# GLA outputs directly behind the out-projection of the head ahead, next queries, keys and log gates behind them

## The chip, the cores and the metric

The kernel runs on one core of one Trainium2 chip. The metric is device time in microseconds (us) of one execution. Engines are named as in the profile: PE is TensorE (matmuls and transposes; PEld its weight loads), ACT is ScalarE, DVE is VectorE, POOL is GpSimd, SP is SyncE, which issues most DMAs. "L151" is line 151 of the kernel.

## The reference

Two layers of width 1024 on a sequence of 512 tokens: an SSD mixer, then a gated linear attention (GLA) mixer, each behind a root-mean-square norm and added to the residual stream, then a last norm. The change lies in the GLA mixer:

```python
def gla_scan(q, k, v, lg):                       # chunks of 64
    def step(s, inp):
        qc, kc, vc, gc = inp
        cum = jnp.cumsum(gc, axis=1)
        qg = qc * jnp.exp(cum)
        kg = kc * jnp.exp(-cum)
        att = jnp.where(causal, jnp.einsum('blhk,bshk->bhls', qg, kg), 0.0)
        o = jnp.einsum('bhls,bshv->blhv', att, vc) + jnp.einsum('blhk,bhkv->blhv', qg, s)
        kd = kc * jnp.exp(cum[:, -1:] - cum)
        s = s * jnp.exp(cum[:, -1])[..., None] + jnp.einsum('bshk,bshv->bhkv', kd, vc)
        return s, o

def gla_mixer(u, w_in, w_gate, b_gate, onorm, w_out):   # 4 heads, keys 128 wide, values 512
    q, k, v, z, gl = split(u @ w_in)
    lg = log_sigmoid(einsum('bldr,drk->bldk', gl, w_gate) + b_gate) / 16
    o = gla_scan(q, k, v, lg[:, :, 0]) + rev(gla_scan(rev(q), rev(k), rev(v), rev(lg[:, :, 1])))
    o = rmsnorm(o, onorm) * silu(z)
    return o @ w_out
```

## The kernel before

Products are done in three matmuls (`mm3`, L150): each operand is split into a high and a low half, a copy on ScalarE and a difference on VectorE. Weights pass through a stream (`Weights`): a chunk is loaded by SyncE (three raw buffers), split (L89 and L90, or L94 and L95 where it is scaled; three buffers), and used in the fixed order in which it was added. `W.next()` splits up to two chunks ahead.

The GLA layer is a loop over four heads (L1119 to L1127). For each head:

- `vz_part`: values and output gates by seven block products (`pb`, 24 matmuls each, two weight chunks each), which write to the four PSUM buffers `mm` and are freed by copies and additions (L889, L903).
- `att_part`: from the summed log gates `lgc` the decayed queries and keys (L999 to L1024, alternating between ScalarE and VectorE), then the attention of all 512 tokens in both directions at once, with masked blocks (`bd`, `pta`), split into `ah` and `al`.
- `proj_out` of the head ahead (`po`, 96 matmuls), reading `gyh` and `gyl`.
- `qk_part` of the next head (`pch`, 48 matmuls, two chunks).
- `gates` of the next head: two matmuls (`ptg`), then for each direction Abs (L959), min (L960), Exp (L963), Ln (L966), a difference (L968) and a running sum (L970).
- `o_part`: for each of four token tiles twelve matmuls (`pto`), a square with its sum (L1092), the root on GpSimd (L318, L319) and the gated product (L1094); then four transposes (`ptyg`, L1078) and a split into `gyh` (ScalarE, L156) and `gyl` (VectorE, L157).

PSUM has four buffers `mm`, three buffers `wk` (`pta`, `ptg`, `pto`) and one buffer `cb` (`bd`, `ptyg`). `gyh`, `gyl` and `lgc` have one buffer each, `gy` two.

The order of each engine's instructions is not the order of the program. A planner lists them by priority, which is the place in the program, shifted where the code says so: weight splits 60 ahead, squares, products and splits of `o_part` 150 ahead, its transposes 24 behind. An instruction is placed when the planner takes its operands to be ready. On the chip each engine then runs its list in that order.

The lines that the change moves:

Of the kernel before, what the change touches and what calls it, by code (L numbers as in the profile page):

```python
# [13 lines left out]
AF = mybir.ActivationFunctionType  # L14
# [14 lines left out]
GH = 4  # L29
# [100 lines left out]
def build(tc, I, out):  # L130
    nc = tc.nc
    ctx = ExitStack()
    with ctx:
# [7 lines left out]
        def mmb(name):  # L141
            return ps.tile([P, 512], F32, tag="mm", name=name, bufs=4)

        def wkb(name):
            return ps.tile([P, 512], F32, tag="wk", name=name, bufs=3)

        def cbb(name):
            return ps.tile([P, 512], F32, tag="cb", name=name, bufs=1)

        def mm3(pt, a, b, first, last):  # L150
            nc.tensor.matmul(pt, lhsT=a[0], rhs=b[0], start=first, stop=False)  # L151
            nc.tensor.matmul(pt, lhsT=a[0], rhs=b[1], start=False, stop=False)  # L152
            W.mm = nc.tensor.matmul(pt, lhsT=a[1], rhs=b[0], start=False, stop=last)  # L153

        def split(hi, lo, src):
            nc.scalar.copy(hi, src)  # L156
            nc.vector.tensor_tensor(out=lo, in0=src, in1=hi.bitcast(F32), op=ALU.subtract)  # L157
# [94 lines left out]
        class Blocks:  # L252
# [8 lines left out]
            def step(self, n):  # L261
                w = self.w
                dst, src, add = (
                    (w["w1"], self.b11, False),
                    (w["w3"], self.b12, False),
                    (w["w1"], self.b12, True),
                    (w["w3"], self.b22, True),
                    (w["w2"], w["w1"], False),
                    (w["w2"], self.b22, True),
                    (w["w4"], w["w2"], False),  # L270
                    (w["w4"], self.b21, True),
                )[n]
                if add:
                    dma = nc.gpsimd.dma_start(dst, src, accum_op=ALU.add)
                else:
                    dma = nc.gpsimd.dma_start(dst, src)
                tc.add_manual_dep(
                    dma.ins, W.mark.ins.name,
                    mybir.DependencyInfo(mybir.DependencyClass.Sync, mybir.DependencyReason.DATA),
                    reason="pace",  # L280
                )
# [35 lines left out]
        def rms(dst, ss, mul, add):  # L317
            nc.gpsimd.tensor_scalar(out=dst, in0=ss, scalar1=mul, scalar2=add, op0=ALU.mult, op1=ALU.add)  # L318
            nc.gpsimd.tensor_tensor(out=dst, in0=dst, in1=nhalf[:, 0 : dst.shape[-1]], op=ALU.pow)  # L319
# [37 lines left out]
        def proj_ch(m=P):  # L357
            wh, wl = W.next()
            pt = mmb("pch")
            for k in range(KD):  # L360
                mm3(pt[0:m], (wh[k], wl[k]), (uh[:, k], ul[:, k]), k == 0, k == KD - 1)
            return pt
# [14 lines left out]
        def proj_out(yts, step=lambda: None):  # L377
            for hf in range(2):
                pts = [mmb(f"po{t}") for t in range(NT)]
                for kk in range(2):  # L380
                    if hf or kk:
                        step()
                    wh, wl = W.next()
                    for t in range(NT):
                        for j in range(2):
                            k = 2 * kk + j
                            mm3(pts[t], yts(k, t), (wh[j], wl[j]), k == 0, k == 3)
                for t in range(NT):
                    hs = h[t][:, hf * 512 : (hf + 1) * 512]
                    nc.vector.tensor_tensor(out=hs, in0=hs, in1=pts[t], op=ALU.add)  # L390
# [49 lines left out]
        with tc.tile_pool(name="sp", bufs=1, reuse_waits="tile") as sp:  # L440
# [347 lines left out]
            zs = {}  # L788
# [37 lines left out]
        with tc.tile_pool(name="gp", bufs=1, reuse_waits="tile") as gp:  # L826
# [124 lines left out]
            def gates(hd):  # L951
                lgc = gp.tile([P, 2, L], F32, tag="lgc", name=f"lgc{hd}")
                ab = []
                for d in range(2):
                    b = bgT[:, d * 4 + hd : d * 4 + hd + 1]
                    pt = wkb("ptg")
                    nc.tensor.matmul(pt, lhsT=wgs[d][:, hd * P : (hd + 1) * P], rhs=gl, start=True, stop=True)
                    a = gp.tile([P, L], F32, tag="ee", name=f"ab{d}", bufs=2)
                    nc.scalar.activation(a, pt, AF.Abs, bias=b)  # L959
                    nc.vector.tensor_scalar(  # L960
                        out=lgc[:, d], in0=pt, scalar1=b, scalar2=0.0, op0=ALU.add, op1=ALU.min
                    )
                    nc.scalar.activation(a, a, AF.Exp, scale=-1.0)  # L963
                    ab.append(a)
                for a in ab:
                    nc.scalar.activation(a, a, AF.Ln, bias=1.0)  # L966
                for d, a in enumerate(ab):
                    nc.vector.tensor_tensor(out=a, in0=lgc[:, d], in1=a, op=ALU.subtract)  # L968
                    lv, av = (lgc[:, d], a) if d == 0 else (lgc[:, d, ::-1], a[:, ::-1])
                    nc.vector.tensor_tensor_scan(  # L970
                        out=lv, data0=rmf, data1=av, initial=0.0, op0=ALU.mult, op1=ALU.add
                    )
                return lgc

            def b4(t):
                return t.rearrange("p (c l) -> p c l", l=P)

            def qk_part(hd):
                q = gp.tile([P, L], F32, tag="q", name=f"q{hd}", bufs=1)
                k = gp.tile([P, L], F32, tag="k", name=f"k{hd}", bufs=1)  # L980
                nc.scalar.mul(q, proj_ch(), float(P) ** -0.5)
                nc.scalar.copy(k, proj_ch())
                return q, k
# [82 lines left out]
            def o_part(hd, att, vs, zs):  # L1066
                yh = gp.tile([P, 4, L], F32R, tag="gyh", name=f"gyh{hd}")
                yl = gp.tile([P, 4, L], F32R, tag="gyl", name=f"gyl{hd}")
                yg[hd] = (yh, yl)
                ys = {}  # L1070

                def trans(t):
                    y = ys.pop(t)
                    sl = slice(t * P, (t + 1) * P)
                    pt = cbb("ptyg")
                    with tc.high_priority(offset=-YG_BEHIND):
                        for f in range(4):
                            nc.tensor.transpose(pt[:, f * P : (f + 1) * P], y[:, f * P : (f + 1) * P], idn)  # L1078
                    with tc.high_priority(offset=YG_AHEAD):
                        split(yh[:, :, sl], yl[:, :, sl], b4(pt))  # L1080

                for t in range(NT):
                    sl = slice(t * P, (t + 1) * P)
                    po = wkb("pto")
                    for J in range(4):
                        ah, al = att[J]
                        mm3(po, (ah[:, sl], al[:, sl]), vs[J], J == 0, J == 3)
                    y = gp.tile([P, 512], F32, tag="gy", name="gy", bufs=2)
                    ss = gp.tile([P, 1], F32, tag="ss", name="ss", bufs=3)
                    rs = gp.tile([P, 1], F32, tag="rs", name="rs", bufs=3)  # L1090
                    with tc.high_priority(offset=YG_AHEAD):
                        nc.scalar.activation(y, po, AF.Square, accum_out=ss)  # L1092
                        rms(rs, ss, 1.0 / 128, 4 * EPS)
                        nc.vector.scalar_tensor_tensor(  # L1094
                            out=y, in0=po, scalar=rs, in1=zs[t // 2][:, t % 2], op0=ALU.mult, op1=ALU.mult
                        )
                    ys[t] = y
                    if t:
                        trans(t - 1)
                trans(NT - 1)  # L1100

            def yts2(hd):
                def f(k, t):
                    yh, yl = yg[hd]
                    sl = slice(t * P, (t + 1) * P)
                    return yh[:, k, sl], yl[:, k, sl]

                return f
# [10 lines left out]
            for hd in range(GH):  # L1119
                vs, zs = vz_part(*([first] if hd == 0 else []))  # L1120
                att = att_part(lgc, *qk)
                if hd:
                    proj_out(yts2(hd - 1))
                if hd + 1 < GH:
                    qk = qk_part(hd + 1)
                    lgc = gates(hd + 1)
                o_part(hd, att, vs, zs)  # L1127
            nb3 = gp.tile([P, D], F32, tag="lgc", name="nb3")
            nc.gpsimd.dma_start(nb3, I["final_norm"].partition_broadcast(P))
            part = {}  # L1130
# [57 lines left out]
```

## Time and profile before

| | us |
|---|---|
| median of three runs | 888.52 |
| lowest and highest | 884.68 and 890.88 |
| profiled execution | 888.3 |
| its span, first to last instruction | 886.6 |
| TensorE busy | 845.9 |
| VectorE busy | 679.4 |
| ScalarE busy | 507.9 |

The mean granted clock of TensorE over the span is 0.989 of full speed. The GLA layer takes the time from about 500 us to the end. Busy time of TensorE is modelled at its end: a matmul of 512 columns is shown with 0.39 us, while the next starts 0.23 us later. So rates are read from starts.

### The profile page before, as it was taken

Reading aid. Unit: us, or ns where it says so; the run is one execution under the profiler, and the core shown is the slowest. Engines: PE = TensorE matmul, PEld = TensorE weight load, DVE = VectorE, ACT = ScalarE, POOL = GpSimd, SP = SyncE. Lnnn points to the kernel's source line nnn. Section 1 sums busy time; section 2 is a strip of 40 time slices with the busy share of each in tenths; the row PEclk is TensorE's granted clock in tenths of the full one; section 3 lists DMA queues with packets and bytes.
Section 4 is the critical chain, followed back from the end, with each engine's and each line's share of the span. In section 5 each row is a group of like instructions: output and inputs, shape, how many; then the busy total and the mean of one; then the engine's idle time right before and its main releaser. Section 6 shows DMA issues by size and latency. Waiting matters only on the chain.

```text
span 886.6 us, 11281 instructions
## 1 busy us (share of the span) xinstructions
PE 845.9 (95%) x3982; PEld 691.4 (78%) x3982; DVE 679.4 (77%) x1046; ACT 507.9 (57%) x1076; POOL 92.8 (10%) x156
## 2 busy tenths in 40 slices
PE   8998989999999999997999999989999999999996
PEld 5787868788887788886887767868887788878875
DVE  6498978999668987568897789878955885588644
ACT  4337687956666466546565547586526653575233
POOL 2002011101001011001101320010001000110012
PEclk9999999999999999998999999999999999999999
DMA  6547856858877687686431236405522453246202
GB/s 207 138 118 280 206 163 194 247 136 262 188 212 214 167 240 191 182 241 166 131 97 58 66 104 186 124 24 162 171 75 69 141 167 95 72 143 189 73 1 95
DMA packets 90198, 132.92 MB, mean 150 GB/s; under 512 B 7969, under 2 KB 49149, under 8 KB 87966
## 3 DMA queue, kind: packets, MB, share of 16 engines
q1 hardware_dynamic: 78716, 97.46, 35.4%
q0 software_dynamic: 11424, 34.74, 16.8%
q8 instruction: 31, 0.51, 0.2%
q14 instruction: 25, 0.20, 0.1%
q10 hardware_dynamic: 2, 0.00, 0.0%
HBM read 129.96 MB, written 35.78 MB: 187 GB/s over the span
## 4 chain that ended last, share of the span: by engine, by line
PE 67%; DVE 11%; ACT 11%; DMA 4%; issue 4%; POOL 3%; SPq 0%; POOLq 0%; ACTq 0%; DVEq 0%
PE po L151 5%; PE po L152 5%; PE pch L152 5%; PE po L153 5%; PE pch L151 5%; PE pch L153 5%; PE pb L151 4%; PE pb L152 4%; PE pb L153 4%; PE pyi L709 3%; DMA bct<-cumd 3%; PE ptk L151 3%; PE ptk L152 3%; PE ptk L153 3%; DVE wlo L90 2%
## 5 line engine op out<-in xcount | busy, mean ns | idle before, releaser
L89 ACT CAST whi<-wraw 128x1024 fp32r<-128x1024 f32 (+1 forms) x114 | 118.7, 1041 | 137.2 <-PE pb L153 43.5
L90 DVE TENSOR_TENSOR wlo<-wraw,whi 128x1024 fp32r<-128x1024 f32 (+1 forms) x114 | 140.4, 1234 | 73.5 <-ACT whi L89 72.9
L151 PE MATMUL pch<-uh,whi 128*128 128x512 f32 (+2 forms) x336 | 133.3, 397 | 0.0
L153 PE MATMUL pch<-uh,wlo 128*128 128x512 f32 (+2 forms) x336 | 132.7, 395 | 0.6 <-DVE wlo L90 0.5
L152 PE MATMUL pch<-ul,whi 128*128 128x512 f32 (+2 forms) x336 | 132.7, 395 | 0.0
L153 PEld LDWEIGHTS pch<-uh,wlo 128*128 128x128 f32 (+2 forms) x336 | 62.6, 186 | 14.9 <-DVE wlo L90 1.5
L152 PEld LDWEIGHTS pch<-ul,whi 128*128 128x128 f32 (+2 forms) x336 | 62.8, 187 | 13.8 <-issue 0.3
L151 PEld LDWEIGHTS pch<-uh,whi 128*128 128x128 f32 (+2 forms) x336 | 62.8, 187 | 13.4
L541 DVE SCALAR_TENSOR_TENSOR cv<-pch,colA,cv 128x511 f32<-128x511 f32 (+1 forms) x96 | 70.7, 742 | 0.3
L94 ACT ACTIVATE whi<-wraw,colB 128x512 fp32r<-128x512 f32 x58 | 39.0, 716 | 53.7 <-PE pch L152 30.0
L318 POOL TENSOR_SCALAR rs<-ss 128x2 f32<-128x2 f32 (+1 forms) x32 | 11.8, 369 | 434.4 <-ACT gy L1092 323.1
L668 ACT ACTIVATE bct<-bct,eb 128x128 f32<-128x128 f32 x128 | 41.3, 392 | 22.0 <-DMA bct<-cumd 22.0
L151 PE MATMUL ptk<-whi,uh 128*128 128x512 f32 x128 | 51.8, 405 | 0.0
L95 DVE SCALAR_TENSOR_TENSOR wlo<-wraw,colB,whi 128x512 fp32r<-128x512 f32 x58 | 41.8, 747 | 11.8 <-ACT whi L94 11.2
L152 PE MATMUL ptk<-wlo,uh 128*128 128x512 f32 x128 | 50.8, 398 | 0.0
L153 PE MATMUL ptk<-whi,ul 128*128 128x512 f32 x128 | 50.6, 396 | 0.0
L676 ACT ACTIVATE bct<-bct,eb 128x128 f32<-128x128 f32 x128 | 41.2, 391 | 6.5 <-DVE bct L673 6.5
L151 PE MATMUL pb<-whi,uh 128*128 128x512 f32 x96 | 39.7, 414 | 2.0 <-DVE u L889 2.0
L707 ACT ACTIVATE xc<-xt,coef 128x64 f32<-128x64 f32 x128 | 33.7, 337 | 10.8 <-DVE coef L629 10.7
L153 PE MATMUL pb<-whi,ul 128*128 128x512 f32 x96 | 39.9, 415 | 0.0
L152 PE MATMUL pb<-wlo,uh 128*128 128x512 f32 x96 | 39.4, 410 | 0.0
L390 DVE TENSOR_TENSOR h<-h,po 128x512 f32<-128x512 f32 x48 | 32.0, 683 | 9.0 <-PE po L153 9.0
(309 smaller groups left out, 2042.0 us busy)
## 6 DMA issues: line engine op xcount, KB each, us to landing
wraw<-in_ssd_w_in_dram SPq DMA_DIRECT2D x48, 512.0 KB, 5.5
wsumw<-in_gla_w_in_dram POOLq DMA_DIRECT2D x24, 1024.0 KB, 9.6
bct<-cumd SPq DMA_DIRECT2D x16, 1024.0 KB, 6.5
wraw<-in_gla_w_in_dram SPq DMA_DIRECT2D x32, 512.0 KB, 3.7
wraw<-wsumw SPq DMA_DIRECT2D x32, 512.0 KB, 3.6
wraw<-in_ssd_w_out_dram SPq DMA_DIRECT2D x16, 512.0 KB, 4.1
wraw<-in_gla_w_out_dram SPq DMA_DIRECT2D x16, 512.0 KB, 3.9
h<-in_x_dram SPq DMA_DIRECT2D x4, 512.0 KB, 7.8
```

What stands on the lines that cost most here:

```text
L89: self.mark = nc.scalar.copy(vh, raw)
L90: nc.vector.tensor_tensor(out=vl, in0=raw, in1=vh.bitcast(F32), op=ALU.subtract)
L94: self.mark = nc.scalar.mul(hs[j], raw[:, j], g)
L95: nc.vector.scalar_tensor_tensor(out=ls[j], in0=raw[:, j], scalar=g, in1=hs[j].bitcast(F32), op0=ALU.mult, op1=ALU.subtract)
L151: nc.tensor.matmul(pt, lhsT=a[0], rhs=b[0], start=first, stop=False)
L152: nc.tensor.matmul(pt, lhsT=a[0], rhs=b[1], start=False, stop=False)
L153: W.mm = nc.tensor.matmul(pt, lhsT=a[1], rhs=b[0], start=False, stop=last)
L390: nc.vector.tensor_tensor(out=hs, in0=hs, in1=pts[t], op=ALU.add)
L541: nc.vector.scalar_tensor_tensor(out=cv[:, o0:o1], in0=pt[:, o0 + s : o1 + s], scalar=cwt(j, a), in1=cv[:, o0:o1], op0=ALU.mult, op1=ALU.add,)
L668: nc.scalar.activation(bct[:, r], bct[:, r], AF.Identity, bias=TM["eb"][:, cc, i : i + 1])
L676: nc.scalar.activation(et[:, r], et[:, r], AF.Exp, bias=TM["eb"][:, cc, i : i + 1])
L707: nc.scalar.mul(xc[:, q, k], xt[:, cc, k], coef[:, cc, r : r + 1])
```

## The change

Two edits. In the loop over heads, `o_part` of heads 1 and 2 moves from behind the next queries, keys and gates to directly behind `proj_out`; in head 0, which has no out-projection ahead, it moves to between `qk_part` and `gates`. Head 3 stays as it is. In `gates`, an order is laid on ScalarE: the two Ln follow the second Exp (`issue_after` makes an instruction follow another in the list of its engine).

```diff
@@ gates
-                    nc.scalar.activation(a, a, AF.Exp, scale=-1.0)
+                    last = nc.scalar.activation(a, a, AF.Exp, scale=-1.0)
                     ab.append(a)
                 for a in ab:
-                    nc.scalar.activation(a, a, AF.Ln, bias=1.0)
+                    with tc.issue_after(last.ins):
+                        last = nc.scalar.activation(a, a, AF.Ln, bias=1.0)
@@ loop over heads
                 att = att_part(lgc, *qk)
                 if hd:
                     proj_out(yts2(hd - 1))
+                    o_part(hd, att, vs, zs)
                 if hd + 1 < GH:
                     qk = qk_part(hd + 1)
+                if not hd:
+                    o_part(hd, att, vs, zs)
+                if hd + 1 < GH:
                     lgc = gates(hd + 1)
-                o_part(hd, att, vs, zs)
```

## Rows read from the trace of the kernel before

**Rows 1.** The page, its first section: busy time, share of the span and instructions of each engine.

```profile
PE 845.9 (95%) x3982; PEld 691.4 (78%) x3982; DVE 679.4 (77%) x1046; ACT 507.9 (57%) x1076; POOL 92.8 (10%) x156
```

**Rows 2.** The timeline of TensorE from 545 to 866 us, rows that have idle time ahead of them (in brackets, with what released them; one such row, of the last out-projection, is left out). Columns: start, duration, engine, line, operation, output and input, shapes, count.

```profile
549.11 0.47 PE L151 MATMUL pb<-whi,uh 128*128 128x512 f32 x1 [2.01 <-DVE u L889]
...
597.48 0.66 PE L1078 MATMUL ptyg<-idn,gy 128*128 128x128 f32 x4 [3.20 <-DVE gyl L157]
...
687.86 0.33 PE L1078 MATMUL ptyg<-idn,gy 128*128 128x128 f32 x1 [1.45 <-DVE gyl L157]
...
691.66 0.66 PE L1078 MATMUL ptyg<-idn,gy 128*128 128x128 f32 x4 [0.17 <-DVE gyl L157]
...
778.97 0.33 PE L1078 MATMUL ptyg<-idn,gy 128*128 128x128 f32 x1 [1.45 <-DVE gyl L157]
...
863.35 0.66 PE L1078 MATMUL ptyg<-idn,gy 128*128 128x128 f32 x4 [0.20 <-DVE gyl L157]
```

**Rows 3.** The timeline of TensorE behind two of these stalls: the first and the last of eight matmuls in a row from 550.40 on, and of nine from 597.89 on.

```profile
550.40 0.63 PE L153 MATMUL pb<-whi,ul 128*128 128x512 f32 x1
...
553.39 0.53 PE L151 MATMUL pb<-whi,uh 128*128 128x512 f32 x1
...
597.89 0.64 PE L152 MATMUL pb<-wlo,uh 128*128 128x512 f32 x1
...
601.32 0.46 PE L151 MATMUL pb<-whi,uh 128*128 128x512 f32 x1
```

**Rows 4.** The timeline of TensorE: the first and the last of the 48 matmuls of queries and keys of head 2.

```profile
660.76 0.39 PE L151 MATMUL pch<-uh,whi 128*128 128x512 f32 x1
...
671.42 0.39 PE L153 MATMUL pch<-uh,wlo 128*128 128x512 f32 x1
```

**Rows 5.** The timeline of ScalarE, with one row of TensorE, from the gates of head 1 to the split of the first output tile of head 0.

```profile
580.85 1.28 ACT L966 ACT_TABLE_LOAD   x1
...
582.79 1.28 ACT L963 ACT_TABLE_LOAD   x1
...
585.31 1.28 ACT L966 ACT_TABLE_LOAD   x1
...
587.25 1.28 ACT L999 ACT_TABLE_LOAD   x1
...
591.60 0.60 PE L1078 MATMUL ptyg<-idn,gy 128*128 128x128 f32 x4
...
595.47 0.63 ACT L1003 ACTIVATE ee<-cm 128x512 f32<-128x512 f32 x1 [1.35 <-DVE cm L1000]
596.01 0.57 ACT L156 CAST gyh<-ptyg 128x512 fp32r<-128x512 f32 x1
```

**Rows 6.** The same place in head 1: the last transpose of the first output tile and what ScalarE did then.

```profile
684.29 0.27 PE L1078 MATMUL ptyg<-idn,gy 128*128 128x128 f32 x1
...
686.08 0.53 ACT L1023 ACTIVATE cm<-cm 128x384 f32<-128x384 f32 x1 [0.28 <-DVE cm L1020]
686.51 0.57 ACT L156 CAST gyh<-ptyg 128x512 fp32r<-128x512 f32 x1
```

**Rows 7.** The same place in head 3, the last head.

```profile
854.17 0.60 PE L1078 MATMUL ptyg<-idn,gy 128*128 128x128 f32 x4
...
854.80 0.59 ACT L156 CAST gyh<-ptyg 128x512 fp32r<-128x512 f32 x1 [1.12 <-PE ptyg L1078]
```

**Rows 8.** The timelines of VectorE and GpSimd: the last low half of the attention of head 1, and the first root of head 3's outputs.

```profile
644.19 0.69 DVE L157 TENSOR_TENSOR al<-pta,ah 128x512 fp32r<-128x512 f32 x1 [0.65 <-ACT ah L156]
...
846.81 0.18 POOL L318 TENSOR_SCALAR rs<-ss 128x1 f32<-128x1 f32 x1 [58.03 <-ACT gy L1092]
```

**Rows 9.** Instructions by line: those of the gates over the whole trace (duration in ns as least/median/most, first and last start in us), and, from the groups of VectorE between 683.26 and 726.07 us (busy us, mean ns, idle before), those of the outputs.

```profile
L959 ACT ACTIVATE ab<-ptg,colB x8: 689/696/714, 532.9 to 764.7; 128x512 f32<-128x512 f32 x8
L963 ACT ACTIVATE ab<-ab x8: 632/638/647, 534.1 to 765.8; 128x512 f32<-128x512 f32 x8
L963 ACT ACT_TABLE_LOAD  x1: 1283/1283/1283, 582.8 to 582.8; - x1
L966 ACT ACTIVATE ab<-ab x8: 622/632/633, 537.5 to 769.6; 128x512 f32<-128x512 f32 x8
L960 DVE TENSOR_SCALAR lgc<-ptg,colB x8: 742/744/751, 534.5 to 765.6; 128x512 f32<-128x512 f32 x8
L968 DVE TENSOR_TENSOR ab<-lgc,ab x8: 668/686/693, 538.6 to 772.3; 128x512 f32<-128x512 f32 x8
L970 DVE TENSOR_TENSOR_SCAN lgc<-rmf,ab x8: 1217/1220/1226, 540.3 to 773.5; 128x512 f32<-128x512 f32 x8
...
L157 DVE TENSOR_TENSOR gyl<-ptyg,gyh 128x512 fp32r<-128x512 f32 x4 | 2.7, 685 | 0.0
L1094 DVE SCALAR_TENSOR_TENSOR gy<-pto,rs,zs 128x512 f32<-128x512 f32 x2 | 1.5, 752 | 0.8 <-POOL rs L319 0.7
```

**Rows 10.** Busy time of each engine in two stretches that lie behind the `pto` matmuls of head 1. Columns: stretch, length, busy us (instructions) of PE, PEld, DVE, ACT and POOL, granted clock, DMA share, GB/s.

```profile
683.26:698.00 14.74, 13.12 (x65) 10.07 (x64) 13.24 (x22) 12.34 (x25) 2.19 (x4) 1.00 0.24 72
698.00:714.53 16.53, 16.53 (x74) 13.69 (x73) 11.69 (x15) 7.37 (x8) 0.00 (x0) 1.00 0.63 188
```

**Rows 11.** The same view of a stretch in head 0, and the VectorE addition in its timeline that released TensorE at 549.11.

```profile
540.00:550.00 10.00, 7.99 (x36) 6.34 (x35) 10.00 (x14) 7.33 (x12) 0.00 (x0) 1.00 0.68 191
...
548.27 1.28 DVE L889 TENSOR_TENSOR u<-pb,u 128x512 f32<-128x512 f32 x2
```

## Prediction

> **What bounds the kernel now.** I read the page first: TensorE is busy for 845.9 us, 95% of the span, VectorE 77% [rows 1]. So time can be won only where TensorE stands still or runs slowly. Next came TensorE's order of time through the GLA layer, keeping only instructions with idle time in brackets [rows 2]. After 545 us there are few, and all but the first are four transposes (`ptyg`, L1078) waiting for `gyl`, the low half of the transposed output of the token tile ahead. All `ptyg` share one PSUM buffer (`cbb`, one buffer), so the transposes of tile t wait until ScalarE (`gyh`) and VectorE (`gyl`) have emptied it of tile t-1. The stalls: 3.20 us in head 0 (597.48), 1.45 and 0.17 us in head 1 (687.86, 691.66), 1.45 us in head 2 (778.97). Head 3 has 0.20 us (863.35).
>
> The first stall costs more than its idle time. Nine matmuls start from 597.89 to 601.32, (601.32-597.89)/8 = 0.43 us apart [rows 3]. In the projection of queries and keys 48 start between 660.76 and 671.42, (671.42-660.76)/47 = 0.227 us apart [rows 4]. The former is the lower of the clock's two levels (1.2 against 2.4 GHz). It costs 8 x (0.43-0.227) = 1.6 us, 1.7 with the four transposes before them. After the 1.45 us stalls the matmuls show no such slowing. What can be won is 3.20 + 1.7 + 1.45 + 0.17 + 1.45 = **8.0 us**.
>
> Then I asked why `gyl` is late: what do ScalarE and VectorE do meanwhile? In head 0, transposes of tile 0 start at 591.60 and take 0.60 us, but `gyh` starts only at 596.01. Ahead of it ScalarE has exponentials of the next head's attention (L1003 at 595.47, itself idle 1.35 us for VectorE), and before these four table loads of 1.28 us at 580.85, 582.79, 585.31 and 587.25, because L963 (Exp) and L966 (Ln) alternate [rows 5]. In head 1 it is the same on a smaller scale: the last transpose of tile 0 starts at 684.29, `gyh` at 686.51, behind L1023 of the next attention at 686.08, which waited for VectorE [rows 6]. In head 3, where nothing of a next head is left, transposes at 854.17 are followed by `gyh` at 854.80 [rows 7]. So the log gates, and the next attention that they release, stand in the way of the outputs.
>
> **The change part by part.**
>
> *Order of heads 1 and 2.* Before: out-projection of the head ahead, queries and keys of the next (48 matmuls, 11.1 us), gates (2 matmuls), outputs. After: out-projection, outputs (48 `pto` matmuls and 16 transposes), queries and keys, gates. No instruction is added or dropped. Can the outputs start 11 us earlier? They need the attention halves `ah`, `al`; the last `al` of head 1 is made at 644.19 and the out-projection runs to 660.76 [rows 4, 8], so 16 us are to spare. They also overwrite `gyh`/`gyl`, which the out-projection reads (one buffer each), but the first such write is a whole `pto` stage later. The tail of the outputs (in head 3 from the first transposes at 854.17 to the last at 863.35, 9.2 us [rows 2, 7]) now lies beside 11 us of query and key matmuls that need two weight splits, and gates and next attention can't get ahead of it, since they follow these matmuls. What is left is head 3's figure, 0.20 us each. Gain: 1.45 + 0.17 + 1.45 - 2 x 0.20 = **2.7 us**.
>
> *Head 0.* Here the outputs pass only the gates. Its `pto` wait for the last `al`, and before, matmuls of the next block product and the gates' two filled that time; now block matmuls alone do, and two chunks of them are split ahead. I cost this at nothing; at worst the gates' two matmuls are not replaced (0.5 us). The squares of tiles 0 and 1 find ScalarE free. Those of 2 and 3 still fall among the gates. The delay left is one activation or one table load, 0.6 to 1.3 us (L963 0.638, load 1.283 [rows 5, 9]); between nothing and head 1's 1.45 I take 0.8. A stall this short left the clock up in head 1, so the slow stretch goes too. Gain: 3.20 + 1.7 - 0.8 = **4.1 us**.
>
> *Both Exp, then both Ln.* Where they alternated (head 0 only) two of the four loads go: 2 x 1.28 = 2.6 us of ScalarE, none of it TensorE time in itself, so zero in the sum; it is inside the 0.8 above. Only one L963 in the whole trace has a load of its own [rows 9], so the other heads have them paired already. The price is that the first Ln waits for the second Exp, thus for the second gate matmul; behind it queue the `gyh` of tiles 1 to 3. They have higher priority (offset 150) and are planned ahead, so I add nothing; at worst this is one load, 1.3 us.
>
> The rows say that Exp and Ln need a load between them, every time. The Trainium skill, ScalarE: Activation LUTs, section "Table sets: the hidden batching unit", says one set holds both, so that Ln after Exp would need no second load. By that the pairing would remove nothing, and head 0 would keep some 2.6 us more delay: gain 4.2 instead of 6.8. The trace disagrees (four loads in 6.4 us), and I follow the trace.
>
> *What arrives at the front of the next block products.* Gates and next attention now compete with weight splits there. From 683.26 to 714.53 VectorE was busy 13.24 + 11.69 = 24.9 of 31.3 us [rows 10]. Out go four `gyl` (2.7) and two L1094 (1.5). In come the gates' two each of L960, L968, L970: 2 x (0.744 + 0.686 + 1.220) = 5.3, less a scan mostly there already (about 1), and a difference of the next attention (L1000, as long as an L968: 0.7) [rows 9]. Net +0.8: 5.6 us stay idle. On ScalarE, 12.34 + 7.37 = 19.7 us, plus 2 x (0.696 + 0.638 + 0.632) + 2.6 = 6.5, less four `gyh` of 0.57 [rows 5]: 23.9. It fits on average, and weight splits keep their priority. Bounds for a head: nothing, as in this stretch of heads 1 and 2 today, or what head 0 pays for gates inside block products. There, VectorE fully busy from 540 to 550, the addition L889 that should free PSUM came at 548.27, TensorE idled 2.01 us, and then eight matmuls started from 550.40 to 553.39, 0.43 us apart, 7 x 0.2 = 1.4 us lost: 3.4 us in all [rows 2, 3, 11]. Head 0 has the splits of the sums of `u` on top, so I take nothing.
>
> DMA: the order of weights is unchanged (outputs use none); the loads of SyncE's queue stay paced by buffers, three deep. On GpSimd L318/L319 move earlier; its one later item is the load of `final_norm` (L1129), which waits for the last gates' buffer and comes later by about the 11 us that they do. Before head 3's L318 at 846.81 that engine has 58.03 us of idle time [rows 8], so it has room.
>
> **Sum.** 2.7 + 4.1 = 6.8 us. The profiled execution took 888.3 us (span 886.6 and 1.7 around it), 0.2 under the median of the three runs, so it stands for them. 888.3 - 6.8 = **881.5 us**, 0.8% less.
>
> **Rivals.**
>
> *A. Head 0 keeps its stall.* If the planner (which fills each engine's order by priority, that is the order of the program shifted by the offsets) still puts the gate matmuls ahead of the last `pto`, as filler while `al` is awaited, gates stay in front of the squares. Against: three `wk` buffers are taken by `pta` and `pto` first. Only heads 1 and 2 gain: 888.3 - 2.7 = 885.6.
>
> *B. Slower: gates and attention clog the front of the block products.* Price: head 0's 3.4 us, in heads 1 to 3: 10.2 - 6.8 = +3.4, 891.7. It decides once an L889 or L90 is queued behind a VectorE step that waits for ScalarE for longer than two block chunks (24 matmuls x 0.227 = 5.4 us). For it: L1003 and L1023 already hold up `gyh` in this way. Against: 5.6 us of slack, and no stall in those stretches now. The Trainium skill, TensorE: Matmul & The Clock Gate, section "Architectural detail: the array is 16× 32×32, not 1× 128×128", says both engines take strictly what is first in the queue. `gyh` behind L1003 agrees with that.
>
> *C. Not what it says.* The transposes are planned by priority (24 behind); if they are simply drawn forward too, the wait for `gyl` recurs among the query matmuls: 888.
>
> *D. More.* The 3.4 us at 549 also vanish because the new edges shift the gates of head 0: 878.1. Nothing in the diff aims at it.
>
> **How the numbers follow.** Forecast 0.58, A 0.14, B 0.13, C 0.08, D 0.07. The three runs lie 0.7% apart, so 1% is about what a measurement can tell from no change. Below 879.6: D, and the forecast with all residues gone (880.3) on a good run: 0.14. Above 897.2: only B with longer stalls: 0.06. Range 878 to 890: it leaves out B and half of D.
>
> **What would show it.** In the new trace: no idle time above 0.5 us on `ptyg` in heads 1 and 2; `gyh` within 1 us of its transposes; ptyg among `pch`; two loads instead of four in head 0's gates; no matmuls 0.43 us apart near 600. It would be wrong if block matmuls (`pb`) that wait for L889 or L90 appear in the 30 us after the gates, or if `pto` of head 1 starts later than its out-projection ends.

## The result and the profile after

The changed kernel takes 880.16 us (median of six runs, 878.35 to 882.64), the kernel before 887.19 (six runs, 884.68 to 890.88): ratio 0.992, 95% interval 0.9899 to 0.9941, so 0.8% less, 7.0 us. Forecast were 881.5 us and 6.8 us. A second measurement of the changed kernel (`e9_after`, below) gave 0.9922 [0.9897, 0.9947].

The page of the profile after, its first lines:

```profile
span 880.3 us, 11269 instructions
PE 845.4 (96%) x3982; PEld 691.6 (79%) x3982; DVE 677.9 (77%) x1046; ACT 505.2 (57%) x1074; POOL 89.3 (10%) x156
```

The span shows 6.3 us of the difference; what lies ahead of the first gate matmul, mostly the SSD layer, took about 1.1 us more in this profiled execution, and the change doesn't touch it. So the two traces are compared over the GLA stretch, from the first gate matmul (`ptg` of head 0) to the end of the last matmul: 349.7 us before and 342.2 us after, 7.5 us less. The columns of these rows, before and after, are those of [rows 10]:

```profile
529.86:879.59 349.73, 340.43 (x1544) 277.64 (x1544) 252.88 (x360) 187.86 (x304) 20.70 (x43) 0.99 0.36 110
...
531.01:873.24 342.23, 338.43 (x1544) 276.41 (x1544) 251.13 (x360) 184.74 (x302) 17.26 (x43) 1.00 0.37 113
```

TensorE's idle time in it went from 9.3 to 3.8 us, and its busy time is 2.0 us less: the slow matmuls went, at the same number of instructions. (Over the whole span busy time differs by only 0.5 us, since the part ahead of the stretch took longer.)

The timeline of TensorE after, again rows with idle time ahead from 545 us on (one row, in the last out-projection, is left out as in [rows 2]):

```profile
550.25 0.47 PE L151 MATMUL pb<-whi,uh 128*128 128x512 f32 x1 [2.01 <-DVE u L889]
...
799.70 0.47 PE L151 MATMUL pb<-whi,uh 128*128 128x512 f32 x1 [0.83 <-ACT whi L89]
...
857.00 0.66 PE L1079 MATMUL ptyg<-idn,gy 128*128 128x128 f32 x4 [0.21 <-DVE gyl L157]
```

Of the six rows of [rows 2] the four waits of transposes in heads 0 to 2 are gone altogether, with the slow matmuls behind the first [rows 3]; the wait in head 0's own block products and head 3's 0.21 us are as they were. One is new: 0.83 us in head 3, ahead of its sixth block product. The account: 3.20 + 1.7 + 1.45 + 0.17 + 1.45 - 0.83 = 7.1 of the 7.5 us; the rest has no row of its own.

Why the waits went, in head 1: the last transpose of tile 0 and the split behind it, then the same in head 0 with the gates' Exp and Ln (TensorE and ScalarE timelines).

```profile
669.53 0.27 PE L1079 MATMUL ptyg<-idn,gy 128*128 128x128 f32 x1
669.84 0.59 ACT L156 CAST gyh<-ptyg 128x512 fp32r<-128x512 f32 x1 [6.01 <-PE ptyg L1079]
...
590.45 0.49 PE L1079 MATMUL ptyg<-idn,gy 128*128 128x128 f32 x3
591.24 0.58 ACT L156 CAST gyh<-ptyg 128x512 fp32r<-128x512 f32 x1
592.29 0.64 ACT L963 ACTIVATE ab<-ab 128x512 f32<-128x512 f32 x1
593.54 0.63 ACT L963 ACTIVATE ab<-ab 128x512 f32<-128x512 f32 x1
596.19 1.28 ACT L967 ACT_TABLE_LOAD   x1
602.48 1.28 ACT L1000 ACT_TABLE_LOAD   x1
```

In head 1 ScalarE had been idle for 6.01 us when the transposes came, where in [rows 6] the split started 2 us after them. In head 0 `gyh` follows within 0.3 us (4 us late in [rows 5]), and two table loads are left of four.

The new wait, in the timelines of ScalarE and VectorE ahead of 799.70:

```profile
796.64 1.05 ACT L89 CAST whi<-wraw 128x1024 fp32r<-128x1024 f32 x1 [1.85 <-DMA wraw<-wsumw]
797.60 0.63 ACT L1004 ACTIVATE ee<-cm 128x512 f32<-128x512 f32 x1
797.73 1.22 DVE L90 TENSOR_TENSOR wlo<-wraw,whi 128x1024 fp32r<-128x1024 f32 x1 [0.90 <-ACT whi L89]
798.13 0.51 ACT L1010 ACTIVATE e<-lgc 128x384 f32<-128x384 f32 x1
798.54 1.03 ACT L89 CAST whi<-wraw 128x1024 fp32r<-128x1024 f32 x1
798.87 1.28 DVE L889 TENSOR_TENSOR u<-pb,u 128x512 f32<-128x512 f32 x2
```

The row of TensorE names L89 as releaser, which can only be the split at 798.54. But counted through the stream, that split is of the seventh product's first chunk; the two of the sixth were split at 793.34 and 796.64. What fits is the addition L889 at 798.87, which frees PSUM: TensorE starts 0.83 us after it, as it starts 0.84 us after the L889 at 548.27 [rows 11]. That addition stood behind L90 at 797.73, which waited 0.90 us for the split at 796.64, and this for its load. SyncE had issued the load at 791.34, when VectorE had finished the low half (L90, 790.10, 1.21 us) that frees its raw buffer. That the busier VectorE frees the raw buffers later, and so delays the load, is a reading that no experiment tested. The wait is no accident of one execution: the other two traces with this order of heads have it too (0.86 us in `e4_order`, 1.14 us in `e9_after`), and no other trace has it.

### The profile page after: what moved, and what is told of

It reads as the page before. It is cut to its first block, busy times and chain, and to the rows that moved or that the text cites. A ratio compares the mean times of both kernels' runs of the same rounds, so it can differ in the third digit from the quotient of the medians.

```text
span 880.3 us, 11269 instructions
## 1 busy us (share of the span) xinstructions
PE 845.4 (96%) x3982; PEld 691.6 (79%) x3982; DVE 677.9 (77%) x1046; ACT 505.2 (57%) x1074; POOL 89.3 (10%) x156
## 4 chain that ended last, share of the span: by engine, by line
PE 69%; DVE 9%; ACT 8%; DMA 6%; issue 4%; POOL 3%; POOLq 0%; ACTq 0%; DVEq 0%; SPq 0%
DMA bct<-cumd 5%; PE pch L152 5%; PE pch L151 5%; PE pch L153 5%; PE po L151 4%; PE po L152 4%; PE po L153 4%; PE pb L151 4%; PE pb L153 4%; PE pb L152 4%; PE pyi L709 3%; PE ptk L151 3%; PE ptk L153 2%; PE ptk L152 2%; DVE wlo L90 2%
## 5 line engine op out<-in xcount | busy, mean ns | idle before, releaser
L90 DVE TENSOR_TENSOR wlo<-wraw,whi 128x1024 fp32r<-128x1024 f32 (+1 forms) x114 | 140.3, 1233 | 52.3 <-ACT whi L89 52.0
L89 ACT CAST whi<-wraw 128x1024 fp32r<-128x1024 f32 (+1 forms) x114 | 118.5, 1040 | 95.2 <-PE pch L152 28.9
L668 ACT ACTIVATE bct<-bct,eb 128x128 f32<-128x128 f32 x128 | 41.3, 391 | 23.9 <-DMA bct<-cumd 23.7
L318 POOL TENSOR_SCALAR rs<-ss 128x2 f32<-128x2 f32 (+1 forms) x32 | 8.2, 258 | 379.5 <-ACT gy L1093 270.2
L153 PE MATMUL pb<-whi,ul 128*128 128x512 f32 x96 | 38.1, 397 | 0.0
L153 PE MATMUL po<-whi,yl 128*128 128x512 f32 x96 | 38.0, 396 | 0.0
```

The source lines that it names most:

```text
L89: self.mark = nc.scalar.copy(vh, raw)
L90: nc.vector.tensor_tensor(out=vl, in0=raw, in1=vh.bitcast(F32), op=ALU.subtract)
L668: nc.scalar.activation(bct[:, r], bct[:, r], AF.Identity, bias=TM["eb"][:, cc, i : i + 1])
```

## Experiments

All are compared with the kernel before, measured beside them (median 888.55 us for the first four, 887.20 for the next four, 886.69 for the last three). "Stretch" is the GLA stretch of one profiled execution, as above. It also holds or lacks the slow matmuls behind the wait at 549 us, which come and go from one execution to the next (last section): the traces of `e3_ln` and `e6_gates_early` lack them, so about 1.6 us of what their stretch is shorter is chance.

**One part at a time.** The first has only heads 1 and 2 in the new order:

```diff
                 if hd:
                     proj_out(yts2(hd - 1))
+                    o_part(hd, att, vs, zs)
                 if hd + 1 < GH:
                     qk = qk_part(hd + 1)
                     lgc = gates(hd + 1)
-                o_part(hd, att, vs, zs)
+                if not hd:
+                    o_part(hd, att, vs, zs)
```

> Only heads 1 and 2 get the new order (outputs directly behind the out-projection); head 0 and the Exp/Ln order stay as before. Theory (the gates and the next attention stood between the transposes and their split): the waits of the transposes in heads 1 and 2 go, 1.45 + 0.17 + 1.45 = 3.1 us, less up to 0.8 us that the whole change has anew in head 3 at its seventh block product: 2.3 to 3.1 us faster, ratio 0.9965 to 0.9974; head 0's 3.2 us stays. Rival (the paired Exp and Ln is what counts): no change, 1.000.

The second has only head 0 in the new order:

```diff
                 if hd + 1 < GH:
                     qk = qk_part(hd + 1)
+                if not hd:
+                    o_part(hd, att, vs, zs)
+                if hd + 1 < GH:
                     lgc = gates(hd + 1)
-                o_part(hd, att, vs, zs)
+                if hd:
+                    o_part(hd, att, vs, zs)
```

> Only head 0 gets the new order (outputs ahead of the gates); heads 1 and 2 and the Exp/Ln order stay as before. Theory: the 3.20 us wait and the 1.7 us of slow matmuls behind it go, 4.9 us, ratio 0.9945, and the 1.45 us waits of heads 1 and 2 stay, though Exp and Ln may alternate with four table loads as before. Rival (the two table loads are what makes head 0 late): 2 us or more of the wait stay, ratio 0.997 or above.

The third has only the Exp/Ln edit:

```diff
-                    nc.scalar.activation(a, a, AF.Exp, scale=-1.0)
+                    last = nc.scalar.activation(a, a, AF.Exp, scale=-1.0)
                     ab.append(a)
                 for a in ab:
-                    nc.scalar.activation(a, a, AF.Ln, bias=1.0)
+                    with tc.issue_after(last.ins):
+                        last = nc.scalar.activation(a, a, AF.Ln, bias=1.0)
```

> Only both Exp, then both Ln; the order of the heads stays as before. Theory: ScalarE saves two loads of 1.28 us in head 0, but the next attention's exponentials still stand ahead of the split, so 1.5 us or more of the 3.20 us wait stay: 0 to 2.6 us faster, ratio 0.997 to 1.000. Rival: the wait and the slow matmuls go entirely, 4.9 us, ratio 0.9945. Heads 1 and 2 keep 1.45 us each by both.

The fourth has the new order of all heads without that edit (shown against the changed kernel):

```diff
-                    with tc.issue_after(last.ins):
-                        last = nc.scalar.activation(a, a, AF.Ln, bias=1.0)
+                    nc.scalar.activation(a, a, AF.Ln, bias=1.0)
```

> The new order of all heads without the Exp/Ln edit. Theory: within 0.5 us of the whole change, ratio 0.992, with no wait of a transpose over 0.5 us; head 0 may show up to four table loads among the splits. Rival: only heads 1 and 2 gain, ratio 0.9965, and a wait of 2 us or more is left in head 0.

| | median, us | ratio, 95% interval | stretch, us | waits in head 0 (transposes; L889 of head 1's products) | in heads 1 and 2 |
|---|---|---|---|---|---|
| before | 888.55 | | 349.7 | 3.20, slow matmuls | 1.45 + 0.17, 1.45 |
| `e1_heads12` | 883.56 | 0.9949 [0.9932, 0.9965] | 345.9 | 3.19, slow matmuls | none |
| `e2_head0` | 884.05 | 0.9950 [0.9931, 0.9968] | 346.9 | 0.87; 1.02 | 1.45, 1.44 |
| `e3_ln` | 883.74 | 0.9953 [0.9934, 0.9971] | 344.1 | 0.77 | 1.44, 1.44 |
| `e4_order` | 880.95 | 0.9926 [0.9908, 0.9945] | 344.3 | 0.84; 1.02 | none |

Some rows of TensorE's timeline on which the table rests: of `e3_ln` (first), of `e2_head0` (next two), of `e4_order` (last two).

```profile
592.73 0.66 PE L1079 MATMUL ptyg<-idn,gy 128*128 128x128 f32 x4 [0.77 <-DVE gyl L157]
```

```profile
599.73 0.44 PE L1078 MATMUL ptyg<-idn,gy 128*128 128x128 f32 x2 [0.87 <-DVE gyl L157]
620.94 0.47 PE L151 MATMUL pb<-whi,uh 128*128 128x512 f32 x1 [1.02 <-DVE u L889]
```

```profile
601.52 0.66 PE L1078 MATMUL ptyg<-idn,gy 128*128 128x128 f32 x4 [0.84 <-DVE gyl L157]
622.72 0.47 PE L151 MATMUL pb<-whi,uh 128*128 128x512 f32 x1 [1.02 <-DVE u L889]
```

Heads 1 and 2 do what the theory said: their waits of 1.45 us go with their own order and not with the other parts. The 0.17 us of head 1 is in no trace but the first, in those of the old order either (`e2_head0`, `e3_ln`), so it can't be put down to the order. By time `e1_heads12` gained 5.0 us, more than the 2.3 to 3.1 expected (the ratio expected, 0.9965, is the end of the interval); by the trace it is 3.8 us against 3.1, and 0.7 us have no row of their own.

Head 0 is where the theory missed. The Exp/Ln edit alone takes 3.20 us down to 0.77 and the slow matmuls away: 2.4 + 1.7 = 4.1 us. The theory had 1.5 us or more staying. Its ratio, 0.9953, lies outside the 0.997 to 1.000 expected, though the interval reaches into it. ScalarE's timeline of `e3_ln`:

```profile
575.61 0.40 PE L957 MATMUL ptg<-gl,wgs 96*128 96x512 f32 x1
...
579.72 1.28 ACT L967 ACT_TABLE_LOAD   x1
...
582.82 1.28 ACT L1000 ACT_TABLE_LOAD   x1
...
589.76 0.60 PE L1079 MATMUL ptyg<-idn,gy 128*128 128x128 f32 x4
590.23 0.52 ACT L1024 ACTIVATE cm<-cm 128x384 f32<-128x384 f32 x1 [0.37 <-DVE cm L1021]
590.66 0.57 ACT L156 CAST gyh<-ptyg 128x512 fp32r<-128x512 f32 x1
...
592.64 0.64 ACT L1004 ACTIVATE ee<-cm 128x512 f32<-128x512 f32 x1
```

The first gate matmul and the transposes of tile 0 are TensorE's. The first gate matmul before:

```profile
577.40 0.39 PE L957 MATMUL ptg<-gl,wgs 96*128 96x512 f32 x1
```

Steps of the next attention still stand ahead of `gyh`, as the theory had it. But `gyh` comes 3.6 us earlier against the first gate matmul (590.66 - 575.61 = 15.1 us; before 596.01 - 577.40 = 18.6), and so 0.3 us after its transposes. Two things account for it. The two loads are 2 x 1.28 = 2.6 us. And the list is another: the last exponential ahead of `gyh` in [rows 5] (L1003, idle for 1.35 us and 0.54 us from its start to that of `gyh`, 1.9 in all) now stands behind it, as L1004 at 592.64. About 0.9 us is lost again between the other steps, mostly to VectorE. No run has one of the two without the other, so what the loads alone are worth stays open; the 4.1 us belong to the edit.

The new order alone (`e2_head0`, `e4_order`) also takes most: it leaves 0.84 to 0.87 us at a transpose and brings 1.02 us for L889. In `e2_head0` the addition L889 which ends that wait starts 31.4 us after the first gate matmul of head 1 (620.11 - 588.76), in the trace after 29.3 (619.48 - 590.14). That the two loads more, 2.6 us, are what makes it late is argued from this. The waits of head 0 with the slow matmuls are thus 4.9 us with neither edit, 0.8 with the pairing, 1.9 with the order, none with both. The two edits treat one wait; their gains don't add. By time `e4_order` is as expected, and 0.9926 can't be told from the 0.9920 and 0.9922 of the whole change: the 1.9 us that the pairing takes off on top of the order are seen in the traces alone, where waits of no more than 0.5 us were expected.

**What of the order matters.** The changed kernel, with head 0's order in heads 1 and 2 as well:

```diff
                 if hd:
                     proj_out(yts2(hd - 1))
-                    o_part(hd, att, vs, zs)
                 if hd + 1 < GH:
                     qk = qk_part(hd + 1)
-                if not hd:
-                    o_part(hd, att, vs, zs)
+                o_part(hd, att, vs, zs)
                 if hd + 1 < GH:
                     lgc = gates(hd + 1)
```

> The changed kernel, but heads 1 and 2 get head 0's order too: out-projection, next queries and keys, outputs, next gates. The tail of the outputs then lies beside block products, as before the change, and only the gates are out of its way. Theory (gates and next attention in the way are the whole cause): no wait of a transpose above 0.5 us in heads 1 and 2, ratio 0.991 to 0.993, as the changed kernel. Rival (the query and key matmuls beside the tail are what counts): 1.45 us come back in each of heads 1 and 2, ratio 0.9955.

The changed kernel, with the gates in front of the outputs in heads 1 and 2:

```diff
                 if hd:
                     proj_out(yts2(hd - 1))
+                    if hd + 1 < GH:
+                        lgc = gates(hd + 1)
                     o_part(hd, att, vs, zs)
                 if hd + 1 < GH:
                     qk = qk_part(hd + 1)
                 if not hd:
                     o_part(hd, att, vs, zs)
-                if hd + 1 < GH:
                     lgc = gates(hd + 1)
```

> The changed kernel, but in heads 1 and 2 the next gates go between the out-projection and the outputs; queries and keys stay behind the outputs, so the gates stand in front of the outputs again, while the next attention can't start. If the steps of the attention are what holds up the split: waits of the transposes in heads 1 and 2 stay under 0.5 us, ratio 0.991 to 0.993. If the gates are: 0.6 to 1.5 us in each of heads 1 and 2, ratio 0.994 to 0.9955.

Measured: `e5_qk_first` 878.75 us, 0.9913 [0.9895, 0.9931], stretch 341.3; `e6_gates_early` 878.86 us, 0.9913 [0.9892, 0.9933], stretch 339.6. Neither has a wait of a transpose in heads 0 to 2, nor the 0.83 us of head 3. By time neither can be told from the changed kernel. So the query and key matmuls as cover are not needed. And in `e6_gates_early` gates ahead of the outputs do no harm. Head 1 of it, ScalarE's timeline with the last transpose of tile 0:

```profile
658.18 1.28 ACT L967 ACT_TABLE_LOAD   x1
...
661.81 1.28 ACT L1000 ACT_TABLE_LOAD   x1
...
666.82 0.19 ACT L1000 ACTIVATE eT<-lgc 128x4 f32<-128x4 f32 x1
667.45 0.27 PE L1079 MATMUL ptyg<-idn,gy 128*128 128x128 f32 x1
667.75 0.59 ACT L156 CAST gyh<-ptyg 128x512 fp32r<-128x512 f32 x1 [0.74 <-PE ptyg L1079]
```

The gates are over before the transposes come; the attention has run only the steps that need no queries or keys, and the split is on time. So in heads 1 and 2 it was the next attention, with its products of queries and keys, that stood ahead of the split.

**The single PSUM buffer.** The kernel before, one edit:

```diff
-                pt = cbb("ptyg")
+                pt = wkb("ptyg")
```

> The kernel before with one edit: the transposes write to the three PSUM buffers of the attention products instead of the single one. Theory: the single buffer only passes on the lateness of the split; with three buffers the waits for the split go in heads 1 and 2 (1.45 us each) and shrink in head 0, but the outputs' matmuls now share the buffers and may wait: ratio 0.992 to 0.999. Rival (the lateness of ScalarE and VectorE alone sets the time): waits of the same sum appear at the outputs or at the next use of the buffers, ratio 1.000.

Measured 885.27 us, 0.9984 [0.9969, 0.9999], stretch 348.0. The waits move: rows of its TensorE timeline from heads 0 and 1.

```profile
593.73 0.50 PE L151 MATMUL pto<-vh,ah 128*128 128x512 f32 x1 [1.23 <-DVE gyl L157]
...
683.60 0.50 PE L151 MATMUL pto<-vh,ah 128*128 128x512 f32 x1 [1.04 <-DVE gyl L157]
691.24 0.63 PE L1078 MATMUL ptyg<-idn,gy 128*128 128x128 f32 x4 [0.57 <-DVE gy L1094]
```

Head 0 has four waits of 0.91 + 0.44 + 1.23 + 0.87 = 3.45 us in place of 3.20, and no slow matmuls behind any of them; heads 1 and 2 have 1.6 us each. The stretch is 1.7 us shorter, as much as the slow matmuls. The late split sets the waits, the buffer only where they are paid, as the rival said; the expected range holds the ratio all the same.

**A faster version.** The wait at 549 us (L889) is for PSUM. The products of q5 and s3 hold all four buffers until the additions behind s3 are done. With s3 ahead, its buffers are emptied while q5 runs:

```diff
-                p5 = block_mm("q5")
                 p7 = block_mm("s3")
                 u3 = [add(keep(i, "u3"), p7[i], u2[i]) for i in two]
+                p5 = block_mm("q5")
...
-                for src in (self.b11, self.b21, w["w2"], w["w1"], w["w3"], w["w4"], self.b22)[a:b]:
+                for src in (self.b11, self.b21, w["w2"], w["w3"], w["w1"], w["w4"], self.b22)[a:b]:
```

On the changed kernel:

> The changed kernel with the fourth and fifth of the seven block products swapped (their weight chunks too): the product of s3 ahead of that of q5, so that its PSUM buffers are emptied while the product of q5 runs. Theory: the wait of 2.01 us for L889 in head 0 is one for PSUM buffers that both products hold; it goes, with the 1.4 us of slow matmuls behind it, and perhaps the 0.83 us of head 3: 2 to 4 us less than the changed kernel, ratio 0.988 to 0.990. Rival (VectorE has too much to do there): a wait of 1.5 us or more appears at a neighbouring product, ratio 0.992.

The same with the early gates of `e6_gates_early`, beside the changed kernel as it is:

> The changed kernel with the two block products swapped and, in heads 1 and 2, the next gates between the out-projection and the outputs. Theory: the gains of the swap (3 to 4 us over the changed kernel) and of earlier gates add up, since the gates no longer press on the front of the block products: ratio 0.986 to 0.989, fastest of all. Rival: the earlier gates give nothing that the swap has not given, ratio 0.989.

> The changed kernel as it is, beside the next two on the same chip. Theory: ratio 0.991 to 0.994 again, and the 0.83 us wait of head 3 (a weight chunk that landed late) may be there or not; no wait of a transpose in heads 0 to 2.

And on the kernel before:

> The kernel before with the two block products swapped and nothing else. Theory: the wait at 549 us and the waits of the transposes are independent: 2.0 to 3.5 us faster, ratio 0.996 to 0.998, and the 3.20 and 1.45 us waits of the transposes stay. Rival: what TensorE gains in head 0 is given back at the transposes of head 0, ratio 1.000.

| | median, us | ratio, 95% interval | stretch, us |
|---|---|---|---|
| `e7_swap` | 875.19 | 0.9886 [0.9865, 0.9907] | 339.1 |
| `e9_after` | 880.49 | 0.9922 [0.9897, 0.9947] | 342.5 |
| `e10_swap_gates` | 876.45 | 0.9883 [0.9860, 0.9906] | 338.4 |
| `e11_swap_only` | 886.44 | 0.9991 [0.9970, 1.0012] | 349.1 |

TensorE's timeline of `e7_swap` has these rows in place of the wait of 2.01 us, its slow matmuls and the 0.83 us:

```profile
560.02 0.91 PE L1042 MATMUL pta<-sc,sc 128*128 128x128 f32 x6 [1.13 <-DVE sc L1007]
...
719.66 0.71 PE L1043 MATMUL pta<-sc,sc 128*128 128x128 f32 x3 [0.29 <-DVE sc L1025]
...
809.39 1.57 PE L1043 MATMUL pta<-sc,sc 128*128 128x128 f32 x8 [0.56 <-DVE sc L1025]
```

Against the trace after, the stretch is 3.1 us less: 0.9 us of idle time (2.01 + 0.83 gone, 1.13 + 0.29 + 0.56 new at the attention, which waits for VectorE) and 2.2 us of busy time (336.2 against 338.4), with the slow matmuls gone. The ratio is in the range expected. The buffers explain the wait; that VectorE is short of time there is true too. Early gates give nothing that can be told from what the swap has given, as the rival said: 0.9883 against 0.9886. Beside `e10_swap_gates` on the same chip the changed kernel (`e9_after`) is 0.4% slower; the intervals just overlap.

On the kernel before the swap alone is not told from no change. Its trace has the 549 us wait gone, but 1.14 us at `pta`, 0.39 at `pto` and 0.15 in each of heads 1 to 3 new, and ten slow matmuls in place of eight behind the transposes' wait of 3.18:

```profile
566.49 0.91 PE L1041 MATMUL pta<-sc,sc 128*128 128x128 f32 x6 [1.14 <-DVE sc L1006]
...
598.25 1.11 PE L1078 MATMUL ptyg<-idn,gy 128*128 128x128 f32 x4 [3.18 <-DVE gyl L157]
```

So the expectation of 2.0 to 3.5 us failed (the interval reaches to 2.7 us, the stretch is 0.6 us shorter). Most of the gain is given back in head 0, at `pta`, `pto` and the transposes.

## Why the prediction was right, and where it was not

*What bounds the kernel, and the 8.0 us to be won*: right, row by row. All of it went. That the sum of 6.8 us came so near the 7.0 measured is in part luck: 0.4 us of residues in heads 1 and 2 and 0.8 in head 0 were forecast and did not come, and 0.83 us in head 3, for which the sum has nothing, did.

*Order of heads 1 and 2, 2.7 us*: the trace shows 3.1, no residue instead of 0.20 per head (0.17 of it is in no other trace). The cause was narrower than stated. The gates were named with the next attention as standing in the way, and the 11 us of queries and keys as cover; `e6_gates_early` acquits the gates and `e5_qk_first` does without the cover.

*Head 0, 4.1 us for the order, and zero in the sum for both Exp, then both Ln*: the total, 4.9 by the trace, was near, but the split was wrong. The pairing alone is worth 4.1 and the order alone about 3.0 (4.9 less 0.87 and 1.02). The step that failed is "none of it TensorE time in itself, so zero in the sum": on top of the order the edit takes 1.9 us of waits away, and alone it brings `gyh` 3.6 us forward, 2.6 of that the loads, and takes 2.4 us off the wait and the slow matmuls with it. The 0.8 us that I left over is what the trace shows with one edit; with both there is none.

*The rule on table sets* (the Trainium skill, ScalarE: Activation LUTs, section "Table sets: the hidden batching unit"): the trace after has two loads in head 0, where Exp and Ln are paired, and `e4_order` four, where they are not. So one set for both is not what this kernel ran with, and the sum by that rule (4.2 us) would have been further off.

*The front of the block products*: forecast were 5.6 us of idle VectorE in 31.3 us and 23.9 us of ScalarE. The same stretch, the front of head 2's block products, after:

```profile
681.49:712.76 31.27, 31.27 (x141) 25.88 (x140) 28.16 (x36) 24.41 (x36) 0.00 (x0) 1.00 0.58 168
```

ScalarE 24.4 is right; VectorE 28.2 leaves 3.1, not 5.6 ([rows 10] for before). The count took in the gates and one step of the attention that moves with them, not the rest. TensorE is busy throughout, so this cost nothing in heads 1 and 2. In head 3 the 0.83 us (1.14 in `e9_after`) is a small piece of rival B, where the forecast had nothing: an L889 queued behind a VectorE step that waited for ScalarE. Its 3.4 us per head did not come.

*Room ahead of the outputs*: 16 us were read from [rows 8]. The attention now runs later, its last `al` of head 1 at 646.39, 10.9 us ahead of the first `pto` at 657.29:

```profile
646.39 0.69 DVE L157 TENSOR_TENSOR al<-pta,ah 128x512 fp32r<-128x512 f32 x1
```

*Rivals*: A is refuted (in head 0 the last `pto` starts at 589.88, the first gate matmul at 590.14, and the wait went). C and D did not come: transposes drawn forward had no wait, and the 2.01 us at 550.25 are still there.

## What to carry to other kernels

Here the waits of the busiest engine were set by what stood ahead of the awaited step in the other engines' lists. So cost every edit that shortens one of these lists by that wait, even if its own engine has idle time on average. Where two edits treat one wait, run each alone before adding their gains: here 4.1 and 3.0 of 4.9 us.

## What the runs showed of the hardware

After the wait of about 2.0 us at 549 us TensorE ran seven or eight matmuls at the lower clock in eight of the ten profiled executions that have this wait. In `e3_ln` and `e6_gates_early` it ran at the full rate straight on, after waits of 2.00 and 2.01 us. Of the latter:

```profile
549.26 0.47 PE L151 MATMUL pb<-whi,uh 128*128 128x512 f32 x1 [2.01 <-DVE u L889]
...
550.04 0.40 PE L151 MATMUL pb<-whi,uh 128*128 128x512 f32 x1
550.27 0.39 PE L152 MATMUL pb<-wlo,uh 128*128 128x512 f32 x1
550.50 0.39 PE L153 MATMUL pb<-whi,ul 128*128 128x512 f32 x1
```

The starts are 0.23 us apart, where [rows 3] has 0.43. So the same wait costs 2.0 or about 3.5 us from one execution to the next. The granted clock (third number from the end) is near half, the lower of the two levels (1.2 of 2.4 GHz), where the matmuls are slow, and full where they are not; the trace before, then `e6_gates_early`:

```profile
550.40:553.82 3.42, 3.42 (x10) 2.73 (x9) 3.29 (x5) 0.61 (x2) 0.00 (x0) 0.52 0.71 198
...
549.26:553.00 3.74, 3.73 (x16) 3.09 (x17) 3.74 (x6) 1.59 (x3) 0.00 (x0) 1.00 0.62 172
```

After waits of 3.2 us the slow matmuls came in all three profiles that have one (before, `e1_heads12`, `e11_swap_only`), after the waits of 1.45 us or less in the GLA stretch in none.
